# The order of weight conversions and half steps in an expert loop, branch hints at its groups, and a tail in pairs

## The chip, the cores and the metric

The kernel runs on one core of a Trainium2 chip. The metric is the device time of one execution in microseconds (us), the median of several runs; less is better.

## The reference

One decoder layer on 1024 tokens of width 1024, in float32: a conditioned normalisation, a mixer (a gated linear recurrence beside sparse attention), and a mixture of experts, which is what this case is about.

```python
N_EXPERTS = 64
TOP_K = 8
EXPERT_HIDDEN = 256

def swiglu(t, w_gu, w_dn):
    g, u = jnp.split(t @ w_gu, 2, axis=-1)
    return (jax.nn.silu(g) * u) @ w_dn
```

Each token goes through a shared expert and through the 8 of 64 experts that a router picks for it. An expert is `swiglu` with `w_gu` of 1024 x 512 and `w_dn` of 256 x 1024; its result is weighted, multiplied by a gate row and added to the token's row. The layer ends with an RMS normalisation of all rows with the gain `final_g`.

## The kernel before

**Columns, groups and kinds.** After the router, the tokens of every expert are packed into *columns*: a column is up to 128 tokens of one expert, a *half column* up to 64. The rows live in DRAM in `h2` (inputs) and `acc` (sums). Columns are put into *groups* of `x + y` columns of two experts: `x` of the one, whose weights stand in slot 0, `y` of the other, in slot 1. Groups of one shape are a *kind*; there are six, `KINDS`, each with `x`, `y`, whether the last column of either expert is a half column, and how many groups there may be. How many there are is known only at run time, so every kind is a nest of `tc.If(ns[kind] > k)` (L1830) around the bodies of its groups (L1831): the program falls through into group k while there is one, and jumps out past the whole nest when there is none. With the inputs of this case 27 groups run: ten of kind 0 (three columns and one, the last column of each expert a half), four of kind 1 (three and one, no half), eight of kind 2 (two and one, the last one a half), four of kind 3 (two and two, each expert's last a half), none of kind 4, one of kind 5 (one and one).

**A step** (`step`, L1961) handles one column. On TensorE (PE): the product of the rows `hTh`, `hTl` (the column's rows turned round, split into a high and a low part) with the weights `guh`, `gul` into `pG` (L1970, L1971, and L1976 if the column is full); in the middle of it, two transposes of the *previous* step's `t` into `pA` (L1926); then the eight transposes of the *next* column's rows `g` into `pX` (L1914, in `turn`); then the down product of the *previous* step, `tTh`, `tTl` with `dnh`, `dnl`, into `pY` (L126 to L128, or L1945 and L1946 for a half). VectorE (DVE) and ScalarE (ACT) split what PE needs: `hTh` (ACT, L1919) and `hTl` (DVE, L1920) from `pX`, `tTh` and `tTl` from `pA` (L1931, L1932), and of the weights, for each piece of 128 x 1024, the high part on ACT (L1904) and the low on DVE (L1905). They also form `t`, the silu of one half of `pG` times the other (for a half column: copy `u` on ACT L1981, two additions on DVE L1983, silu on ACT L1984, multiplication on DVE L1985), and the weighted output `y` (L1952 to L1958).

**The order.** Every engine runs its queue in the order written. The six pieces of a slot's weights (q0 to q3 of `w_gu`, q4 and q5 of `w_dn`) are loaded by SyncE into `raw`, and each is converted at a fixed place: `SPLITTING` has for every step of a group two strings, the pieces that are converted after the `gu` product is issued (`now`) and those at the step's end (`late`). `a4`, `a5` are left from the group before, `b0` to `b5` are the second expert's of this group, `n0` to `n5` the first expert's of the next. GpSimd (POOL) gathers rows for a later column (L1880) and adds the outputs into `acc` (L1886), one after another.

**The end.** After the last kind a drain ends the last column, and `final` (L2004 on) loads `acc` in eight tiles `xl`, takes the sums of squares on ACT (L2019), the inverse roots on DVE in a chain of small operations (L136 to L141), scales in three groups of three, three and two tiles (L2029 to L2032) and stores (L2034).

Of the kernel before, what the change touches and what calls it, by code (L numbers as in the profile page):

```python
# [7 lines left out]
F32 = mybir.dt.float32  # L8
# [3 lines left out]
AF = mybir.ActivationFunctionType  # L12
OP = mybir.AluOpType
# [4 lines left out]
D = 1024  # L18
T = 1024
NT = 8  # L20
KT = 8
EPS = 1e-6
# [5 lines left out]
         (2, 2, (True, True), 32, 276, 4), (2, 2, (False, False), 32, 132, 4), (1, 1, (False, False), 32, 406, 2))  # L28
S1, S2, S3, S4, S5, S6 = (x[4] for x in KINDS)
NC = 474  # L30


def turned(x):
# [6 lines left out]
def consts():  # L40
# [27 lines left out]
    pad = np.stack([1024 + p, 0 * p], 1).reshape(256)  # L68
    row = np.concatenate([low, e * 1024 + 1, pad, np.arange(NC)]).astype(f)[None]
    j = np.arange(4)  # L70
# [11 lines left out]
def flip(x, i):  # L82
# [25 lines left out]

SPLITTING = {(3, 1): ("a4 a5", "b0", "b1 b2", "b3", "b4", "b5 n0", "n1 n2", "n3"),
# [3 lines left out]


ORDER = (3, 2, 1, 0, 4, 5, 6, 7)
# [2 lines left out]
class K:  # L120
# [77 lines left out]
    def pool(self, st, name, bufs, **k):  # L198
        return st.enter_context(self.tc.tile_pool(name=name, bufs=bufs, reuse_waits="tile", **k))
# [741 lines left out]
    def rows(self):  # L941
# [7 lines left out]
        G.memset(self.sacc, 0.0)  # L949
        self.krow = row(a["k_row"], 384 + NC, "krow")  # L950
        self.g1r = row(self.mods[0:1], D, "g1r")
# [528 lines left out]
    def chain(self, t):  # L1480
# [209 lines left out]
        yield  # L1690
        hot = t.tile([128, 4, NC], F32R, name="hot")
        for j in range(4):
            V.tensor_scalar(hot[:, j], self.krow[:, 384:384 + NC], col[:, j:j + 1], None, op0=OP.is_equal)

        def look(rows, *parts):

            ps = psum()[:rows, :NC]
            n = len(parts) * 4
# [35 lines left out]
    def phase3(self, ctx):  # L1734
        tc, nc, a = self.tc, self.nc, self.a
        V, S, G, P = nc.vector, nc.scalar, nc.gpsimd, nc.tensor
        pool = self.pool
        big = ExitStack()
# [3 lines left out]
        with tc.manual_schedule():  # L1742
# [45 lines left out]
            m = pool(big, "moe", 1, side="right")  # L1788
# [4 lines left out]
            self.y = [m.tile([128, D], F32, name=f"y{s}") for s in range(2)]  # L1793
            self.idx = m.tile([128, NC], I32, name="idx")
            self.wgt = m.tile([128, NC], F32, name="wgt")
# [10 lines left out]
            tail = ExitStack()  # L1806
# [21 lines left out]
            ns = [nc.values_load(self.num[0:1, k:k + 1], min_val=0, max_val=KINDS[k][3]) for k in range(6)]  # L1828
            for kind, (_, _, half, most, c0, way) in enumerate(KINDS):
                with ExitStack() as nest:  # L1830
                    for k in range(most):  # L1831
                        self.prev = self.last(64 if k and half[1] else 128)
                        nest.enter_context(tc.If(ns[kind] > k))
                        self.group(kind, c0 + k * way)
            self.prev = self.last(128)
            self.drain()
            tail.close()
            self.final(pool(big, "last", 1, side="right"))
            big.close()

    def group(self, kind, c):
# [7 lines left out]
        f = {f"a{k}": self.todo[k] for k in (4, 5)}  # L1849
        at = iter(SPLITTING[x, y])  # L1850
        for u, (slot, cols) in enumerate(units):
# [109 lines left out]
    def step(self, slot, load, now, late, store, half=False, ahead=False):  # L1961


        nc = self.nc
        V, S, G, P = nc.vector, nc.scalar, nc.gpsimd, nc.tensor
        s = self.par
        gu = self.W[slot][0][0], self.W[slot][1][0]
        hT, ps = self.hT2[s], self.pG[s]
        for k in range(KT):
            P.matmul(ps, hT[0][:, k], gu[0][:, k], start=(k == 0), stop=False)  # L1970
            P.matmul(ps, hT[0][:, k], gu[1][:, k], start=False, stop=(half and k == KT - 1))  # L1971
            if k == 1 and self.prev:
                self.middle()
        if not half:
            for k in range(KT):
                P.matmul(ps, hT[1][:, k], gu[0][:, k], start=False, stop=(k == KT - 1))  # L1976
        for f in now:
            f()
        if half:
            t, u = self.t[:64], self.u  # L1980
            S.activation(u, ps[64:], AF.Copy)  # L1981
            for c in (slice(0, 256), slice(256, 512)):
                V.tensor_tensor(u[:, c], u[:, c], ps[:64, c], op=OP.add)  # L1983
            S.activation(t, u[:, :256], AF.Silu)  # L1984
            V.tensor_tensor(t, t, u[:, 256:], op=OP.mult)  # L1985
            self.turn(1 - s, ahead)
        else:
            S.activation(self.t, ps[:, :256], AF.Silu)
            V.tensor_tensor(self.t, self.t, ps[:, 256:], op=OP.mult)
            self.turn(1 - s, ahead)  # L1990
        if load:
            load(self.g[1 - s])
        if self.prev:
            self.down(self.pslot)
        for f in late:
            f()
        self.prev, self.pslot = store, slot
        self.par = 1 - s
# [5 lines left out]
    def final(self, m):  # L2004

        nc = self.nc
        V, S, G = nc.vector, nc.scalar, nc.gpsimd
        tok = [slice(i * 128, (i + 1) * 128) for i in range(NT)]
        self.fg = self.bcast(m, self.a["final_g"].rearrange("(a n) -> a n", a=1), D, "fg")
        xs = [m.tile([128, D], F32, name=f"xl{i}") for i in range(NT - 2)] + self.g  # L2010
        for i in range(NT):
            nc.sync.dma_start(xs[i], self.acc[tok[i]])
        groups = (0, 1, 2), (3, 4, 5), (6, 7)
        sums = [m.tile([128, len(tiles)], F32, name=f"ss{j}") for j, tiles in enumerate(groups)]
        r = {}

        def squares(j):
            for u, i in enumerate(groups[j]):
                S.activation(self.pY, xs[i], AF.Square, accum_out=sums[j][:, u:u + 1])  # L2019

        def root(j):
            ss = sums[j]
            V.tensor_scalar(ss, ss, 1.0 / D, EPS, op0=OP.mult, op1=OP.add)
            r[j] = self.rsqrt(m, ss, len(groups[j]), f"fr{j}")

        def scale(j):
            for u, i in enumerate(groups[j]):
                if u == 2:
                    S.activation(xs[i], xs[i], AF.Copy, scale=r[j][:, u:u + 1])  # L2029
                    G.tensor_tensor(xs[i], xs[i], self.fg, op=OP.mult)  # L2030
                else:
                    V.scalar_tensor_tensor(xs[i], xs[i], r[j][:, u:u + 1], self.fg, op0=OP.mult, op1=OP.mult)  # L2032
            for i in groups[j]:
                nc.sync.dma_start(self.out[0, tok[i]], xs[i])  # L2034

        squares(0)
        squares(1)
        root(0)
        scale(0)
        squares(2)  # L2040
        root(1)
        scale(1)
        root(2)
        scale(2)


def body(tc, a, out, dbg=None, upto=9):
# [33 lines left out]
```

## Time and profile before

| | us |
|---|---|
| median of 3 runs (2010.75 to 2018.43) | 2016.76 |
| the profiled execution | 2016.18 |
| its span in the trace | 2014.4 |
| expert groups, from the start of the first to the end of the last | 1037 to 1979 |
| the tail, from the last scatter to the end | 1980.8 to 2014.4 |

The profile is of one execution. Busy time is given by engine; PE's weight loads (PEld) overlap its matmuls. In its rows a name after an L is a line of the kernel, `out<-in` the tiles written and read, and "[1.25 <-ACT hTh L1919]" means that the engine had stood idle for 1.25 us until that instruction released it. "DVEq" and "PEldq" stand for an engine's sequencer: an engine that is named so was released by a branch or semaphore instruction.

### The profile page before, as it was taken

The page shows a single profiled execution, that of the slowest core. Times are in us where ns is not written, and L with a number is a line of the kernel's source. Part 1 is how long each engine was busy: PE and PEld are TensorE (multiplying, and loading weights), DVE is VectorE, ACT ScalarE, POOL GpSimd, SP SyncE. Part 2 cuts the span into 40 slices and gives each one's busy share as a digit, 9 for nine tenths or more (in the row PEclk, how much of TensorE's full clock was granted, in tenths as well). Part 3 has the DMA queues.
Part 4 walks back from the last instruction along what each step waited for, and adds up shares of the span by engine and source line. Part 5 has one row for each costly group of instructions (what it writes and reads, how often), then busy time and mean ns, then how long its engine had stood idle before and what let it go on. Part 6 is the DMA issues. An engine that isn't in the chain of part 4 may idle for free. (4 is left out here: it accounts for less than half of the span.)

```text
span 2014.4 us, 29910 instructions
## 1 busy us (share of the span) xinstructions
PE 1795.7 (89%) x10534; PEld 1519.9 (75%) x10534; DVE 1416.7 (70%) x2397; ACT 1002.8 (50%) x1685; POOL 759.9 (38%) x644
## 2 busy tenths in 40 slices
PE   3989889899998999997899898998999999989972
PEld 3878879898887799886777777776887777766751
DVE  5577687624866676655767888887676788877765
ACT  4544545433743454444135556564454666655542
POOL 5155666612234443323523333333333333333322
PEclk9999998999999899998999999998999999999986
DMA  7413242332411111104489888886986999978855
GB/s 252 129 50 108 63 129 92 96 114 85 159 63 43 43 43 38 38 12 144 77 262 286 269 235 261 239 263 174 300 252 169 357 313 301 290 241 251 235 156 195
DMA packets 184279, 343.80 MB, mean 171 GB/s; under 512 B 24508, under 2 KB 83136, under 8 KB 184064
## 3 DMA queue, kind: packets, MB, share of 16 engines
q1 hardware_dynamic: 154768, 268.82, 39.5%
q0 software_dynamic: 29200, 72.41, 16.2%
q8 instruction: 95, 1.56, 0.3%
q14 instruction: 120, 0.98, 0.2%
q10 hardware_dynamic: 96, 0.02, 0.0%
HBM read 300.72 MB, written 65.36 MB: 182 GB/s over the span
## 5 line engine op out<-in xcount | busy, mean ns | idle before, releaser
L1970 PE MATMUL pG<-guh,hTh 128*128 128x512 f32 x848 | 353.9, 417 | 64.0 <-ACT hTh L1919 33.9
L1971 PE MATMUL pG<-gul,hTh 128*128 128x512 f32 x848 | 344.1, 406 | 15.2 <-DVE gul L1905 14.2
L1886 POOL DMA_INDIRECT acc<-y,idx x71 | 146.7, 2066 | 353.6 <-DVE dnl L1905 88.6
L1905 DVE TENSOR_TENSOR gul<-raw,guh 128x1024 fp32r<-128x1024 f32 x224 | 267.2, 1215 | 2.1 <-ACT guh L1904 2.1
L1970 PEld LDWEIGHTS pG<-guh,hTh 128*128 128x128 f32 x848 | 164.1, 194 | 107.3 <-ACT hTh L1919 44.0
L1904 ACT ACTIVATE guh<-raw 128x1024 fp32r<-128x1024 f32 x224 | 229.0, 1050 | 3.1 <-DMA raw<-w_exp_gu 2.5
L1971 PEld LDWEIGHTS pG<-gul,hTh 128*128 128x128 f32 x848 | 164.4, 194 | 58.1 <-DVE gul L1905 26.0
L127 PE MATMUL pj<-wl,hTh 128*128 128x256 f32 (+1 forms) x576 | 165.2, 287 | 5.8 <-DVE wl L224 5.8
L126 PE MATMUL pj<-wh,hTh 128*128 128x256 f32 (+1 forms) x576 | 169.5, 294 | 0.2 <-ACT wh L223 0.2
L1880 POOL DMA_INDIRECT g<-h,idx x101 | 117.6, 1165 | 135.1 <-PE pX L1914 113.4
L128 PE MATMUL pj<-wh,hTl 128*128 128x256 f32 (+1 forms) x576 | 164.6, 286 | 0.0
L1295 PE MATMUL po<-v,pT 128*128 128x64 f32 x1056 | 137.9, 275 | 11.0 <-DVE ob L1309 6.6
L1263 ACT ACTIVATE p<-ps,nm 128x640 f32<-128x640 f32 (+7 forms) x128 | 89.9, 702 | 114.6 <-DVE nm L1261 112.8
L1295 PEld LDWEIGHTS po<-v,pT 128*128 128x128 f32 x1056 | 132.8, 194 | 15.4 <-issue 6.6
L1976 PE MATMUL pG<-guh,hTl 128*128 128x512 f32 x560 | 141.5, 394 | 0.0
L1905 DVE TENSOR_TENSOR dnl<-raw,dnh 128x1024 fp32r<-128x1024 f32 x110 | 132.9, 1232 | 2.1 <-ACT dnh L1904 2.1
L1920 DVE TENSOR_TENSOR hTl<-pX,hTh 128x1024 fp32r<-128x1024 f32 x71 | 86.9, 1224 | 58.7 <-ACT hTh L1919 54.2
L1976 PEld LDWEIGHTS pG<-guh,hTl 128*128 128x128 f32 x560 | 105.4, 188 | 24.9
L126 PE MATMUL pY<-dnh,tTh 128*128 128x512 f32 x292 | 123.0, 421 | 0.5 <-ACT tTh L1931 0.5
L128 PE MATMUL pY<-dnh,tTl 128*128 128x512 f32 x292 | 117.2, 402 | 0.0
L127 PEld LDWEIGHTS pj<-wl,hTh 128*128 128x128 f32 x576 | 111.6, 194 | 6.8 <-DVE wl L224 6.7
L127 PE MATMUL pY<-dnl,tTh 128*128 128x512 f32 x292 | 115.8, 396 | 0.0
(486 smaller groups left out, 4394.5 us busy)
## 6 DMA issues: line engine op xcount, KB each, us to landing
raw<-w_exp_gu SPq DMA_DIRECT2D x220, 512.0 KB
raw<-w_exp_dn SPq DMA_DIRECT2D x110, 512.0 KB
raw<-w_ada SPq DMA_DIRECT2D x24, 1024.0 KB
x<-x SPq DMA_DIRECT2D x16, 512.0 KB
raw<-w_in SPq DMA_DIRECT2D x16, 512.0 KB
raw<-w_in SPq DMA_DIRECT2D x5, 1024.0 KB
acc<-x SPq DMA_DIRECT2D x9, 512.0 KB
h<-y SPq DMA_DIRECT2D x8, 512.0 KB
```

The source lines that it names most:

```text
L126: mm(ps, l[0], r[0], start=first, stop=False)
L127: mm(ps, l[0], r[1], start=False, stop=False)
L128: mm(ps, l[1], r[0], start=False, stop=last)
L1263: nc.scalar.activation(p[:, :n], ps[:, :n], AF.Exp, bias=nm, accum_out=self.st[i]["sums"][:, h, br + 1:br + 2])
L1295: self.nc.tensor.matmul(self.po[:, h % 2, br], pt[:, u * 128:(u + 1) * 128], self.vst[br][:, a + u, g * 64:g * 64 + 64], start=(u == 0), s ...
L1880: return lambda g: nc.gpsimd.indirect_dma_start(out=g[:n, :], out_offset=None, in_=self.h2, in_offset=off, bounds_check=T - 1, oob_is_err= ...
L1886: return lambda y: nc.gpsimd.indirect_dma_start(out=self.acc, out_offset=off, in_=y[:n, :], in_offset=None, compute_op=OP.add, bounds_chec ...
L1904: S.activation(h[:, o:o + 1024], x, AF.Copy)
L1905: V.tensor_tensor(l[:, o:o + 1024], x, h.bitcast(F32)[:, o:o + 1024], op=OP.subtract)
L1970: P.matmul(ps, hT[0][:, k], gu[0][:, k], start=(k == 0), stop=False)
L1971: P.matmul(ps, hT[0][:, k], gu[1][:, k], start=False, stop=(half and k == KT - 1))
L1976: P.matmul(ps, hT[1][:, k], gu[0][:, k], start=False, stop=(k == KT - 1))
```

## The change

Five edits:

1. `SPLITTING`: in groups of 3 + 1, step 3 converts b4 now and n0, n1 late, step 4 n2, n3 now and b5 late; before, step 3 had b4 now, b5 and n0 late, step 4 n1, n2 now and n3 late. The other shapes change likewise.
2. In a half step, `turn` (the transposes and conversion of the next column's rows) is written ahead of the silu and the multiplication that form `t`.
3. Every `tc.If` gets a label, and each but a nest's last is followed by a branch hint for the next one, on five engines, with a register that is 1 when the program will jump at that next `If`, 0 when it will go on into its group. On every engine this puts two instructions behind the branch of a group: a comparison and the hint.
4. The pool `last` is opened before the drain, and the last `y` gets a tile of its own.
5. `final` loads and stores by the SyncE and ACT queues in turn, takes all squares first, and works in four pairs on DVE, with no scaling on ACT and POOL.

```diff
-SPLITTING = {(3, 1): ("a4 a5", "b0", "b1 b2", "b3", "b4", "b5 n0", "n1 n2", "n3"),
-             (2, 1): ("a4 a5 b0", "b1", "b2 b3", "b4 n0", "b5 n1 n2", "n3"),
-             (2, 2): ("a4 a5", "b0", "b1 b2", "b3", "b4 b5", "n0", "n1 n2", "n3"),
-             (1, 1): ("a4 a5 b0 b1", "b2 b3", "b4 b5 n0 n1", "n2 n3")}
+SPLITTING = {(3, 1): ("a4 a5", "b0", "b1 b2", "b3", "b4", "n0 n1", "n2 n3", "b5"),
+             (2, 1): ("b0 a4 a5", "b1", "b2 b3", "n0 n1", "n2 n3", "b4 b5"),
+             (2, 2): ("b0 a4 a5", "b1", "b2 b3", "n0", "b4 b5", "n1", "n2 n3", ""),
+             (1, 1): ("b0 b1 b2", "b3 a4 a5", "n0 n1 n2", "n3 b4 b5")}
...
-                        nest.enter_context(tc.If(ns[kind] > k))
+                        nest.enter_context(tc.If(ns[kind] > k, label=f"{kind}.{k}"))
+                        if k + 1 < most:
+                            tc.mark_branch_hint_location(f"{kind}.{k + 1}", hint=ns[kind] <= k + 1, engines=ENGINES)
                         self.group(kind, c0 + k * way)
             self.prev = self.last(128)
+            tail.close()
+            m = pool(big, "last", 1, side="right")
+            self.y[self.par] = m.tile([128, D], F32, name="yl")
             self.drain()
-            tail.close()
-            self.final(pool(big, "last", 1, side="right"))
+            self.final(m)
...
+            self.turn(1 - s, ahead)
             S.activation(t, u[:, :256], AF.Silu)
             V.tensor_tensor(t, t, u[:, 256:], op=OP.mult)
-            self.turn(1 - s, ahead)
...
-            nc.sync.dma_start(xs[i], self.acc[tok[i]])
-        groups = (0, 1, 2), (3, 4, 5), (6, 7)
...
+            (nc.sync, nc.scalar)[i % 2].dma_start(xs[i], self.acc[tok[i]])
+        pairs = [(i, i + 1) for i in range(0, NT, 2)]
+        sums = [m.tile([128, 2], F32, name=f"ss{j}") for j in range(NT // 2)]
+        for j, tiles in enumerate(pairs):
+            for u, i in enumerate(tiles):
                 S.activation(self.pY, xs[i], AF.Square, accum_out=sums[j][:, u:u + 1])
...
+        for j, tiles in enumerate(pairs):
+            V.tensor_scalar(sums[j], sums[j], 1.0 / D, EPS, op0=OP.mult, op1=OP.add)
+            r = self.rsqrt(m, sums[j], 2, f"fr{j}")
+            for u, i in enumerate(tiles):
+                V.scalar_tensor_tensor(xs[i], xs[i], r[:, u:u + 1], self.fg, op0=OP.mult, op1=OP.mult)
+                (nc.sync, nc.scalar)[u].dma_start(self.out[0, tok[i]], xs[i])
```

What stands on DVE in a group of kind 0, from the late conversions of its third step to the end of its fourth, the half step (`raw` to `gul` or `dnl` is a weight conversion, `u` and `t` are the half step's products, `hTl` the next column's rows, `y` the previous column's output). Before:

```order
L1905 TENSOR_TENSOR dnl_9407<-raw_10470,dnh_9406 128x1024
L1905 TENSOR_TENSOR gul_10479<-raw_9599,guh_10478 128x1024
L1932 TENSOR_TENSOR tTh<-pA,tTh 128x2x64
L1905 TENSOR_TENSOR gul_10479<-raw_9599,guh_10478 128x1024 x2
L1983 TENSOR_TENSOR u<-u,pG_9394 64x256 x2
L1985 TENSOR_TENSOR t<-t,u 64x256
L1920 TENSOR_TENSOR hTl_9564<-pX,hTh_9563 128x1024
L1953 TENSOR_TENSOR y_9572<-y_9572,pY 64x1024
L1954 SCALAR_TENSOR_TENSOR y_9572<-y_9572,wgt,g2r 64x1024
L1905 TENSOR_TENSOR gul_10479<-raw_9599,guh_10478 128x1024
```

The same place on DVE with the change:

```order
L1910 TENSOR_TENSOR gul_10479<-raw_9599,guh_10478 128x1024 x2
L1937 TENSOR_TENSOR tTh<-pA,tTh 128x2x64
L1910 TENSOR_TENSOR gul_10479<-raw_9599,guh_10478 128x1024 x2
L1988 TENSOR_TENSOR u<-u,pG_9394 64x256 x2
L1925 TENSOR_TENSOR hTl_9564<-pX,hTh_9563 128x1024
L1991 TENSOR_TENSOR t<-t,u 64x256
L1958 TENSOR_TENSOR y_9572<-y_9572,pY 64x1024
L1959 SCALAR_TENSOR_TENSOR y_9572<-y_9572,wgt,g2r 64x1024
L1910 TENSOR_TENSOR dnl_9407<-raw_10470,dnh_9406 128x1024
```

The `dnl` conversion has gone from the first place to the last, all four `gul` conversions stand ahead of the additions, and `hTl` stands ahead of the multiplication that ends `t`.

On ACT, the same half step before:

```order
L1931 ACTIVATE tTh<-pA 128x2x64
L1904 ACTIVATE guh_10478<-raw_9599 128x1024 x2
L1981 ACTIVATE u<-pG_9394 64x512
L1984 ACTIVATE t<-u 64x256
L1919 ACTIVATE hTh_9563<-pX 128x1024
L1952 ACTIVATE y_9572<-pY 64x1024
L1904 ACTIVATE guh_10478<-raw_9599 128x1024
```

And on ACT with the change:

```order
L1936 ACTIVATE tTh<-pA 128x2x64
L1909 ACTIVATE guh_10478<-raw_9599 128x1024 x2
L1986 ACTIVATE u<-pG_9394 64x512
L1924 ACTIVATE hTh_9563<-pX 128x1024
L1990 ACTIVATE t<-u 64x256
L1957 ACTIVATE y_9572<-pY 64x1024
L1909 ACTIVATE dnh_9406<-raw_10470 128x1024
```

`hTh`, which the next step's first matmul reads, now stands ahead of the silu `t<-u`, which waits for DVE's additions.

DVE at the start of kind 0's second group, where the hints come in. Before:

```order
L1830 COMPARE_AND_BRANCH
L1932 TENSOR_TENSOR tTh<-pA,tTh 128x2x64
L1905 TENSOR_TENSOR dnl_10481<-raw_9599,dnh_10480 128x1024 x2
L1989 TENSOR_TENSOR t<-t,pG_9393 128x256
L1920 TENSOR_TENSOR hTl_9566<-pX,hTh_9565 128x1024
```

And with the change:

```order
L1831 COMPARE_AND_BRANCH
L1836 REGISTER_ALU
L2061 BRANCH_PREFETCH_HINT
L1937 TENSOR_TENSOR tTh<-pA,tTh 128x2x64
L1910 TENSOR_TENSOR dnl_10481<-raw_9599,dnh_10480 128x1024 x2
L1994 TENSOR_TENSOR t<-t,pG_9393 128x256
```

Behind the branch stand the comparison and the hint, the same on each of the five engines, and then the group as before.

More of the change, by code (lines that the diff above doesn't have):

```diff
@@ L30 @@
 NC = 474
+ENGINES = [getattr(mybir.EngineType, x) for x in ("PE", "Activation", "DVE", "Pool", "SP")]
 def turned(x):
@@ L2011, in final @@
         for i in range(NT):
-            nc.sync.dma_start(xs[i], self.acc[tok[i]])
-        groups = (0, 1, 2), (3, 4, 5), (6, 7)
[L2014 to L2044, printed above, removed]
+            (nc.sync, nc.scalar)[i % 2].dma_start(xs[i], self.acc[tok[i]])
[3 more added lines that the diff above has]
+            for u, i in enumerate(tiles):
+                S.activation(self.pY, xs[i], AF.Square, accum_out=sums[j][:, u:u + 1])
+        for j, tiles in enumerate(pairs):
[4 more added lines that the diff above has]
+                (nc.sync, nc.scalar)[u].dma_start(self.out[0, tok[i]], xs[i])
 def body(tc, a, out, dbg=None, upto=9):
```

## The prediction

> **What bounds the kernel now.** I read the page first (busy time), then PE's waits in the expert stage, then the busy time by stretches, one group of each kind, and last the order of time at the stalls.
>
> ```profile
> span 2014.4 us, 29910 instructions
> PE 1795.7 (89%) x10534; PEld 1519.9 (75%) x10534; DVE 1416.7 (70%) x2397; ACT 1002.8 (50%) x1685; POOL 759.9 (38%) x644
> ```
>
> PE is busy 89% of the span, the others far less. Next, whom PE waited for from 1037 to 1979 us, the expert stage (sum, how often, the longest):
>
> ```profile
> PE pG L1970 <- ACT hTh L1919: 31.7, 22, 1.6
> PE pG L1970 <- DVEq L1830: 29.5, 4, 12.6
> PE pG L1971 <- DVE gul L1905: 14.2, 11, 2.2
> PE pA L1926 <- DVEq L1830: 3.8, 1, 3.8
> ```
>
> And five stretches of that stage (length, then busy time with counts of PE, weight load, DVE, ACT, POOL, then PE's clock, DMA share, GB/s): a group of kind 0, one of kind 1, the first of kind 2, another of kind 2, one of kind 3.
>
> ```profile
> 1284.30:1319.70 35.40, 32.85 (x163) 25.75 (x162) 29.01 (x37) 20.78 (x28) 12.60 (x8) 1.00 0.85 249
> 1437.50:1475.40 37.90, 37.90 (x187) 31.06 (x185) 26.78 (x31) 18.56 (x25) 12.40 (x8) 1.00 0.90 258
> 1558.60:1583.40 24.80, 24.76 (x113) 19.92 (x114) 15.71 (x18) 13.71 (x18) 5.52 (x5) 0.93 1.01 345
> 1666.70:1694.50 27.80, 26.11 (x128) 20.56 (x127) 24.37 (x30) 17.89 (x24) 8.97 (x6) 1.00 0.98 306
> 1857.70:1894.40 36.70, 33.49 (x162) 25.44 (x161) 29.05 (x37) 20.78 (x28) 14.08 (x9) 1.00 0.81 238
> ```
>
> PE is the bound, full in kind 1 (37.90 of 37.90) and with 2.55, 1.69 and 3.21 us of holes in kinds 0, 2 and 3. The wait rows name the holes: 31.7 us for `hTh` in 22 places, 14.2 us for `gul` in 11, and 33.3 us (29.5 + 3.8) at the five places where the program jumps out of a kind's nest. All else that the change touches is the tail. The time to be won in the expert stage is these 79 us and no more.
>
> **The half step.** What its stall is made of, in order of time, where kind 0's half step passes into the next group:
>
> ```profile
> 1178.13 2.35 DVE L1905 TENSOR_TENSOR gul<-raw,guh 128x1024 fp32r<-128x1024 f32 x2
> 1178.19 1.03 PE L1914 MATMUL pX<-ident,g 128*128 128x128 f32 x8
> 1180.40 0.74 DVE L1983 TENSOR_TENSOR u<-u,pG 64x256 f32<-64x256 f32 x2
> 1180.71 0.40 PE L1946 MATMUL pY<-dnl,tTh 128*128 128x512 f32 x1
> 1180.84 0.42 ACT L1984 ACTIVATE t<-u 64x256 f32<-64x256 f32 x1 [1.86 <-DVE u L1983]
> 1181.28 1.02 ACT L1919 ACTIVATE hTh<-pX 128x1024 fp32r<-128x1024 f32 x1
> 1181.29 0.42 DVE L1985 TENSOR_TENSOR t<-t,u 64x256 f32<-64x256 f32 x1 [0.15 <-ACT t L1984]
> 1182.34 1.23 DVE L1920 TENSOR_TENSOR hTl<-pX,hTh 128x1024 fp32r<-128x1024 f32 x1 [0.63 <-ACT hTh L1919]
> 1182.36 0.50 PE L1970 MATMUL pG<-guh,hTh 128*128 128x512 f32 x1 [1.25 <-ACT hTh L1919]
> 1183.39 0.38 PE L1926 MATMUL pA<-ident,t 128*128 128x128 f32 x2
> 1184.72 1.28 DVE L1954 SCALAR_TENSOR_TENSOR y<-y,wgt,g2r 64x1024 f32<-64x1024 f32 x1
> 1185.92 1.21 DVE L1905 TENSOR_TENSOR gul<-raw,guh 128x1024 fp32r<-128x1024 f32 x1
> 1187.18 0.50 PE L1971 MATMUL pG<-gul,hTh 128*128 128x512 f32 x1 [1.31 <-DVE gul L1905]
> ```
>
> `pX` is ready at 1179.22, but `hTh` stands on ACT behind the silu, which waited 1.86 us for the `u` adds, themselves behind two conversions on DVE. So `hTh` ends at 1182.30 and PE, done at 1181.11, waits 1.25. With the turn moved ahead, `hTh` runs at 1179.3 to 1180.3 and this wait is gone. What is late next is `t`: DVE does `hTl` (1.23) ahead of the multiplication. The adds end at 1181.14, `hTl` at 1182.37, `t` (0.42) at 1182.8 or, with the 0.05 to 0.15 us that such handovers take, 1182.95. PE, starting at 1181.11, reaches `pA` after the 1.03 us that lie between 1182.36 and 1183.39, at 1182.14: a **new wait of 0.8 us** where there was none. Net gain 1.25 - 0.8 = 0.45.
>
> **The order of the pieces.** The last row's 1.31 us is n3's `gul`, converted late, behind `hTl` and the two `y` operations (1184.72 to 1186.0). In the new order n2 and n3 stand together ahead of the adds, where the old order also had two conversions (the 2.35), and b5, a `dn` piece wanted only by the down product of the next step, takes the late place. So this wait goes without a successor. Kind 0 has ten groups (1037 to 1390.4), nine boundaries inside: 9 x (0.45 + 1.31) = **15.8 us**. Bounds: 0, if another wait fills both, and 23 (9 x 2.56), if `t` isn't late.
>
> **Kind 2.** Its eight groups have seven such boundaries:
>
> ```profile
> 1660.54 1.46 POOL L1886 DMA_INDIRECT acc<-y,ci  x1 [6.35 <-DMA acc<-y,idx]
> 1662.73 1.28 DVE L1958 SCALAR_TENSOR_TENSOR y<-pY,wgt,g2r 128x1024 f32<-128x1024 f32 x1 [1.21 <-PE pY L128]
> 1671.89 0.50 PE L1970 MATMUL pG<-guh,hTh 128*128 128x512 f32 x1 [1.61 <-ACT hTh L1919]
> ```
>
> 7 x 1.61 = 11.3 us, here with no new wait, since `n2 n3` no longer stand between the adds and `t`. But the stretch row has DMA at 0.98 of 27.80 us: if those 27.2 us can't shrink, 0.6 a boundary is all, 4.2 us. Against that, the kind's first group moved 345 GB/s, 13% over the 306 of the stretch, which would carry the whole 1.61. I take **7**, between the ends 4.2 and 11.3.
>
> **Kind 3 and kind 1.** What is left of the 31.7 us is 31.7 - 11.25 - 11.3 = 9.2 us at six half steps of kind 3, 1.5 each; by the sum above each keeps a `pA` wait of 0.8 to 1.1, which leaves **2.5** to 4 us; I take the lower, as these steps carry two half columns. Kind 1 has no half step and PE without a hole: 0.
>
> **The exits.** PE stops there while DVE runs its queue dry. The branches of all five places and of the groups between (count, least, middle and longest ns):
>
> ```profile
> L1830 PEldq COMPARE_BRANCH  x38: 65/65/5802, 1037.0 to 1969.0; - x38
> L1830 DVEq COMPARE_BRANCH  x38: 43/43/67, 1042.2 to 1972.6; - x38
> ```
>
> And the first exit in order of time:
>
> ```profile
> 1392.78 0.40 PE L1946 MATMUL pY<-dnl,tTh 128*128 128x512 f32 x1
> 1399.19 0.14 DVE L1864 COPY cw<-wgt 128x1 f32<-128x1 f32 x1
> 1400.23 0.76 PE L1970 MATMUL pG<-guh,hTh 128*128 128x512 f32 x1 [7.06 <-DVEq L1830]
> ```
>
> PE's branch takes 65 ns when it falls through into the next group and up to 5.8 us when it jumps. The jump hides behind DVE: its last instruction ends at 1399.33, PE goes on at 1400.23. Even a free jump gains 0.9 us here, and about 3.7 over the five places. The new order shifts one late conversion (1.2 us) into kind 2's exit and one out of kind 3's: 0 net. The added instructions (one compare, one hint, for each of 27 groups and engine) at 65 ns each come to 3.5 us if nothing hides them; PE's sequencer runs ahead of its matmuls, so I take **0** for their issue, bounds 0 and +3.5. [...]
>
> **The tail.**
>
> ```profile
> 1988.33 1.03 ACT L2019 ACTIVATE pY<-xl 128x1024 f32<-128x1024 f32 x1
> 1991.76 0.17 DVE L2023 TENSOR_SCALAR ss<-ss 128x3 f32<-128x3 f32 x1 [11.26 <-DMA xl<-acc]
> 1996.73 2.33 DVE L136 TENSOR_SCALAR fr1t<-ss 128x3 int32<-128x3 int32 x1
> 2001.06 4.65 DVE L2032 SCALAR_TENSOR_TENSOR xl<-xl,fr1y,fg 128x1024 f32<-128x1024 f32 x2
> 2007.99 2.48 DVE L2032 SCALAR_TENSOR_TENSOR g<-g,fr2y,fg 128x1024 f32<-128x1024 f32 x2
> ```
>
> Now three roots (some 2.37 us each, 1991.76 to 1994.14) and six scalings end at 2010.47. After, with pairs, the chain starts two squares in (1989.6, the second ends at 1989.36), and holds 4 x 2.37 + 8 x 1.24 = 19.4 us on DVE, so it ends at 2009.0, **-1.4**; the 2.17 us on each of two DVE operations that ran beside POOL's multiplication (2.33 where its like took 0.17, 4.65 where it took 2.48) go with POOL's part. Opening the last pool ahead of the drain, with a tile of its own for the last `y`, moves nothing that I can see, since the loads read `acc` and so wait for the last scatter as before: 0. Two queues for eight loads may land the first pair later; bounds -2 and +1, taken **-1**. [...]
>
> **Sum.** 15.8 + 7 + 2.5 + 1 = 26 us from the profiled execution's 2016.2 (the median of the runs is 2016.8, 0.03% off, so no correction): 1990. The scatters, next, can hold some of it back; I leave 3 us for them: **1993**, own range 1982 (2016.2 - 23 - 11.3, kinds 0 and 2 at their bounds) to 2003 (half the sum).
>
> **Rivals.**
>
> [...]
>
> [...]
>
> [...]
>
> *The scatters take the stall's place.* POOL's additions into `acc` go one after the other: at 1660.54 it waited 6.35 us for the scatter before, and the next `y` is written at 1662.73, 2.2 us behind. If the scatter chain, not PE, sets the period of kind 2 and the half groups, only that margin is won, once, with half of the `gul` waits of kind 0 (9 x 1.31 / 2 = 5.9) and the tail: 2016.2 - 2.2 - 5.9 - 1 = **2007**. For it: every kind 2 scatter waits for a landing. Against it: PE's row names no wait for `y`.
>
> *The jumps become short* because the hints bring the target in: 3.7 us more, **1989**. For it: PE's jumps are 3.6 to 5.8 us. Against it: DVE, not PE, ends last there; and the sense of the register would have to be the other.
>
> *The hints do nothing* is the forecast itself.
>
> **How the numbers follow.** Forecast 0.43, short jumps 0.07, scatters 0.16, code loading 0.34. About 0.5%, or 10 us, is what a measurement of this kernel can tell from no change: 2006 to 2026 counts as same. Faster: 0.42 + 0.07 + 0.04 = 0.53; same: 0.01 + 0.10 + 0.05 = 0.16; slower: 0.02 + 0.29 = 0.31. The range goes down to the forecast's lower bound with the short jumps' 3.7 us, 1982 - 4 = 1978, and up into the code loading case as far as leaves out no more than 2 in 10: 2046.
>
> **What would show it.** Right: `hTh` waits gone, `pA` waits of 0.8 us on `t` in kind 0, `gul` waits gone but for the first, kind 0 groups at 33.6 us, kind 2 near 26.8. [...] Scatters: PE or ACT waiting for `acc<-y`. It would be wrong from the start if `t` or the new late b5 comes much later than counted.

## The result, and the profile after

The changed kernel takes 1983.78 us in the median of four runs (1979.6 to 1984.11), the kernel before 2016.71 in the same measurement: a ratio of 0.984, 95% interval 0.982 to 0.986. The profiled execution took 1979.6 us, the fastest of the four. Its page:

```profile
span 1977.8 us, 30098 instructions
PE 1785.2 (90%) x10534; PEld 1517.6 (77%) x10534; DVE 1409.0 (71%) x2411; ACT 999.0 (51%) x1683; POOL 755.6 (38%) x642
```

PE's busy time is 10.5 us less for the same 10534 matmuls. PE's waits in the expert stage (who waited for whom, sum, how often, the longest):

```profile
PE pG L1975 <- DVEq L1831: 24.4, 4, 10.9
PE pA L1931 <- DVE t L1991: 12.5, 16, 1.3
PE pA L1931 <- DVEq L1831: 5.7, 1, 5.7
PE pX L1919 <- DMA g<-h,idx: 4.2, 2, 2.3
PE pY L1950 <- DVE tTh L1937: 3.0, 1, 3.0
PE pY L129 <- DVE tTl L1937: 2.8, 1, 2.8
PE pG L1976 <- DVE gul L1910: 2.6, 2, 2.2
PE pA L1931 <- DVE t L1994: 1.4, 1, 1.4
```

The 31.7 us for `hTh` are gone without a rest, the `gul` waits but for the first and one of 0.4 us in kind 5. New are sixteen `pA` waits for the `t` of a half step, one for that of a full column, and two single waits of about 3 us, which the section on the hints takes up. The stretches of a group of kind 0, one of kind 2, one of kind 3, and of the fifth group of kind 0 (length, busy time and counts of PE, weight load, DVE, ACT, POOL, then PE's clock, DMA share, GB/s):

```profile
1276.25:1309.34 33.09, 32.47 (x161) 25.79 (x161) 28.51 (x37) 20.67 (x29) 11.95 (x8) 1.00 0.86 264
1667.50:1693.16 25.66, 25.66 (x128) 20.63 (x127) 24.09 (x30) 17.85 (x23) 8.35 (x5) 1.00 0.99 323
1797.55:1832.15 34.60, 32.84 (x160) 25.55 (x160) 28.74 (x37) 20.79 (x28) 11.92 (x9) 1.00 0.90 252
1172.98:1210.05 37.07, 32.71 (x160) 25.81 (x161) 28.64 (x37) 20.66 (x29) 13.52 (x10) 1.00 0.87 253
```

The groups went from 35.4, 27.8 and 36.7 us to 33.1, 25.7 and 34.6, and PE's rows fill all 25.66 us of kind 2's group. The order of time where kind 0's half step passes into the next group:

```profile
1305.94 1.03 ACT L1924 ACTIVATE hTh<-pX 128x1024 fp32r<-128x1024 f32 x1 [0.28 <-PE pX L1919]
1307.08 0.74 DVE L1988 TENSOR_TENSOR u<-u,pG 64x256 f32<-64x256 f32 x2
1307.62 0.40 PE L1975 MATMUL pG<-guh,hTh 128*128 128x512 f32 x1
1307.74 1.21 DVE L1925 TENSOR_TENSOR hTl<-pX,hTh 128x1024 fp32r<-128x1024 f32 x1
1308.32 0.40 PE L1976 MATMUL pG<-gul,hTh 128*128 128x512 f32 x1
1308.87 0.41 DVE L1991 TENSOR_TENSOR t<-t,u 64x256 f32<-64x256 f32 x1
1309.34 0.44 PE L1931 MATMUL pA<-ident,t 128*128 128x128 f32 x2 [0.62 <-DVE t L1991]
```

`hTh` is done at 1306.97, 0.65 us before PE reads it; `t` is what PE now waits for, behind `hTl`: 0.62 to 0.67 us at eight of the nine boundaries of kind 0, and 1.32 us at the one behind the group of 37.07 us.

### The profile page after: what moved, and what is told of

Its sections match the earlier page's. It is cut to its first block, busy times and chain, and to the rows that moved or that the text cites. A ratio compares the mean times of both kernels' runs of the same rounds, so it can differ in the third digit from the quotient of the medians.

```text
span 1977.8 us, 30098 instructions
## 1 busy us (share of the span) xinstructions
PE 1785.2 (90%) x10534; PEld 1517.6 (77%) x10534; DVE 1409.0 (71%) x2411; ACT 999.0 (51%) x1683; POOL 755.6 (38%) x642
## 5 line engine op out<-in xcount | busy, mean ns | idle before, releaser
L1975 PE MATMUL pG<-guh,hTh 128*128 128x512 f32 x848 | 349.8, 413 | 27.2 <-DVEq L1831 24.4
L1976 PE MATMUL pG<-gul,hTh 128*128 128x512 f32 x848 | 339.9, 401 | 2.6 <-DVE gul L1910 2.6
L1885 POOL DMA_INDIRECT g<-h,idx x101 | 125.1, 1239 | 118.5 <-PE pX L1919 92.5
L1936 ACT ACTIVATE tTh<-pA 128x256 fp32r<-128x256 f32 (+1 forms) x106 | 37.2, 351 | 163.8 <-PE pA L1931 141.4
```

The costliest lines, as they stand in the source:

```text
L1885: return lambda g: nc.gpsimd.indirect_dma_start(out=g[:n, :], out_offset=None, in_=self.h2, in_offset=off, bounds_check=T - 1, oob_is_err= ...
```

## The experiments

The table holds every kernel: its median, the ratio to the kernel before on the same chip with its 95% interval, and in its single trace the length of the expert stage, from the end of PE's first `gul` wait to the `pA` transposes behind the last exit. What lies ahead of that stage is the same code in all, and yet the stage begins anywhere from 1036 to 1043 us in these traces; so its length is a cleaner measure of a single trace than the span. It scatters too: e9 has the same code in that stage as the kernel before, and its stage is 3.8 us shorter. Medians of different rows may come from different chips; rows are compared by their ratios.

| kernel | median us | ratio (interval) | expert stage us |
|---|---|---|---|
| before | 2014.4 to 2017.1 | 1 | 932.4 |
| the change | 1983.8 | 0.984 (0.982 to 0.986) | 899.5 |
| e1 change without hints | 1974.1 | 0.981 (0.979 to 0.983) | 892.3 |
| e2 before, hints alone | 2033.6 | 1.010 (1.008 to 1.012) | 945.3 |
| e3 change, hints reversed | 1966.8 | 0.977 (0.975 to 0.978) | 885.6 |
| e4 before, turn alone | 1994.3 | 0.990 (0.989 to 0.992) | 908.5 |
| e5 change, hints always 1 | 1975.6 | 0.980 (0.978 to 0.983) | 893.0 |
| e6 change, no hints on DVE | 1973.6 | 0.979 (0.977 to 0.982) | 890.1 |
| e7 change, hints on DVE alone | 1989.3 | 0.986 (0.984 to 0.988) | 906.8 |
| e8 before, pieces and turn | 1977.1 | 0.982 (0.979 to 0.984) | 890.3 |
| e9 before, tail alone | 2016.9 | 1.000 (0.999 to 1.001) | 928.6 |
| e10 before, pieces alone | 1993.1 | 0.989 (0.987 to 0.990) | 906.8 |
| e11 e3 with `t` ahead of `hTl` | 1958.6 | 0.972 (0.970 to 0.973) | 872.4 |
| e12 e11 without hints | 1964.5 | 0.975 (0.973 to 0.977) | 884.9 |

### The hints

Three theories stood after the result: the hints do nothing; they pay, since PE's jumps had become short (0.35 to 0.38 us at the exits of kinds 0 to 3, where 3.6 to 5.8 had been); they cost, since DVE had stood still twice inside a group (3.89 us at 1203 and 3.98 at 1643). "Late code" in the expectations is the author's guess at what DVE stood still for; no row shows it. **e1** leaves them out:

```diff
-                        nest.enter_context(tc.If(ns[kind] > k, label=f"{kind}.{k}"))
-                        if k + 1 < most:
-                            tc.mark_branch_hint_location(f"{kind}.{k + 1}", hint=ns[kind] <= k + 1, engines=ENGINES)
+                        nest.enter_context(tc.If(ns[kind] > k))
```

> The changed kernel without its hints (edits 1, 2, 4 and 5 alone). If the hints do nothing for the time, 1984 us. If they pay by the short jumps, it is slower by what the exits lost in the changed kernel's trace, about 3 us: 1987, with PE's branch at 3.6 to 5.8 us again at every exit and PE's holes there back to 7.1, 3.9, 6.0 and 12.6 us. If they cost by late code, it is faster: DVE stood still twice for 3.9 us in the middle of a group (at 1203 and 1643 us) with all its operands there, and without hints both stops are gone, 1976.

**e2** is the kernel before with the hints of the change and nothing else.

> The kernel before with the hints alone. Hints nothing: 2016.7. Short jumps pay: 2013, PE's branches at the exits of kinds 0 to 3 under 0.4 us and the holes there shorter. Late code: 2020 to 2025, with stops of DVE of about 4 us inside groups.

**e3** turns the register's sense round in the changed kernel:

```diff
-hint=ns[kind] <= k + 1
+hint=ns[kind] > k + 1
```

> The changed kernel with the sense of the hint's register turned: 1 where the program goes on, 0 where it jumps. If 1 means 'bring in the target', as the short jumps of the changed kernel suggest, 22 hints are now wrong: PE stops inside groups, 2 us each in the middle, 2025 or so, and the jumps take 3.6 to 5.8 us again. If the register's value does nothing, it equals the changed kernel: 1984.

Without hints the kernel is some 6 us faster by the ratios, 0.981 against 0.984, but their intervals overlap a little. The kernel before makes it plain: hints alone cost it 1.0%, some 20 us, with the whole interval above 1, and more than the 2020 to 2025 us expected. So in the change the hints cost, and the other edits gave more than the result shows. e3 came out against its expectation, both of whose branches gave at least the time of the change: the reversed sense is faster than no hints at all, 0.977 against 0.981. Whether PE's jumps are short is read from its branches. At the exit of kind 0 (count, least, middle and longest ns), in the changed kernel:

```profile
L1831 PEldq COMPARE_BRANCH  x3: 65/190/382, 1372.7 to 1376.0; - x3
```

in e1:

```profile
L1831 PEldq COMPARE_BRANCH  x3: 73/193/3365, 1370.5 to 1374.4; - x3
```

and in e3:

```profile
L1831 PEldq COMPARE_BRANCH  x3: 65/195/421, 1368.1 to 1371.4; - x3
```

Both senses make that jump short, 0.38 and 0.42 us against 3.4. Kind 5 tells them apart, since only one of its groups runs and so only one hint. The change, where that hint has the value 1:

```profile
L1831 PEldq COMPARE_BRANCH  x2: 193/3140/6086, 1928.5 to 1934.8; - x2
```

e3, where it has 0:

```profile
L1831 PEldq COMPARE_BRANCH  x2: 186/277/368, 1915.1 to 1918.9; - x2
```

With 1 the jump took 6.1 us, with 0 0.37, and without hints (e1) 5.9. So **0 is the value that makes the jump short**. In the change the 22 groups that go on have the value 0 and the last group of each kind has 1; the jumps behind the last groups of kinds 0 to 3, each with zeros in the groups before, were short all the same, 0.35 to 0.38 us. **e5** puts this to the test, with the same instructions at the same places but the value always 1:

```diff
-hint=ns[kind] <= k + 1
+hint=ns[kind] <= 40
```

> The changed kernel with the hint's register always 1, so the same instructions at the same places, but in no group the value 0. If the value decides and 0 means 'bring in the target of the jump', this does nothing: the time of the kernel without hints, 1974, with PE's jumps at 3.4 to 5.9 us again. If it is the shifted code or the extra instructions that made the reversed hints 7 us faster than none, it is 1967. If 1 also loads something, PE or DVE stop inside groups: 1984.

It equals no hints, 0.980 against 0.981, with stage lengths 893.0 and 892.3, and its jumps are long again (5.9 us in kind 5). So neither the extra instructions nor the shifted code make a difference that this measurement can tell: the value does. **e6** and **e7** ask which engine pays, with these lines:

```diff
-engines=ENGINES
+engines=[e for e in ENGINES if e != mybir.EngineType.DVE]
```

and

```diff
-engines=ENGINES
+engines=[mybir.EngineType.DVE]
```

> The changed kernel with its hints on PE, ACT, POOL and SP, none on DVE. If the cost of the 22 hints with 0 is DVE's late code alone, the stops are gone: 1974, or 1972 with short jumps on the other engines. If the other engines' code is late too, it stays near 1984; in between, each takes its share.

> The changed kernel with its hints on DVE alone. If DVE's late code is the cost: 1982 to 1984, stops of DVE of about 4 us inside groups, PE's jumps long. If the cost is elsewhere: 1974 or less.

The cost is DVE's: without its hints 0.979, with them alone 0.986, intervals well apart. That e7 lies above the change itself and above the 1982 to 1984 us expected may mean that the other engines' hints give something back there; the intervals of e7 and of the change overlap, so it is not shown. Three stops in the changed kernel, DVE's rows (the second row is the last work ahead of the second stop):

```profile
1125.99 1.28 DVE L1963 SCALAR_TENSOR_TENSOR y<-pY,wgt,g2r 128x1024 f32<-128x1024 f32 x1 [3.28 <-PE pA L1931]
1197.88 1.28 DVE L1963 SCALAR_TENSOR_TENSOR y<-pY,wgt,g2r 128x1024 f32<-128x1024 f32 x1 [1.33 <-PE pY L129]
1203.05 2.36 DVE L1910 TENSOR_TENSOR gul<-raw,guh 128x1024 fp32r<-128x1024 f32 x2 [3.89 <-ACT u L1986]
1642.95 2.36 DVE L1910 TENSOR_TENSOR gul<-raw,guh 128x1024 fp32r<-128x1024 f32 x2 [3.98 <-DMA raw<-w_exp_gu]
```

The same places in e7:

```profile
1132.80 1.28 DVE L1963 SCALAR_TENSOR_TENSOR y<-pY,wgt,g2r 128x1024 f32<-128x1024 f32 x1 [4.18 <-issue]
1209.75 2.36 DVE L1910 TENSOR_TENSOR gul<-raw,guh 128x1024 fp32r<-128x1024 f32 x2 [4.03 <-ACT u L1986]
1649.07 2.36 DVE L1910 TENSOR_TENSOR gul<-raw,guh 128x1024 fp32r<-128x1024 f32 x2 [3.91 <-ACT u L1986]
```

And e2, where another conversion stands behind the same `y`, again in the fifth group of kind 0:

```profile
1210.12 1.23 DVE L1908 TENSOR_TENSOR dnl<-raw,dnh 128x1024 fp32r<-128x1024 f32 x1 [4.09 <-ACT u L1984]
1293.17 1.21 DVE L1956 TENSOR_TENSOR y<-y,pY 64x1024 f32<-64x1024 f32 x1 [4.46 <-issue]
```

And ACT in the changed kernel, ahead of the stop at 1203.05:

```profile
1195.68 2.00 ACT L1909 ACTIVATE guh<-raw 128x1024 fp32r<-128x1024 f32 x2
```

DVE's `y` ended at 1199.16 and its conversion began at 1203.05, though ACT had written `guh` for it by 1197.68; the releasers named (ACT's `u`, PE's `pA`, a DMA) are only what happened last, and twice it is "issue", that is, nothing that the profile shows. The change and e7 stop at the same instructions of the same groups, a `y` in kind 0's third group, a `gul` in its fifth and a `gul` in one group of kind 2. The other groups of kind 0 pass these instructions without such a stop, and e1, e5 and e6 pass all three places (the same `y` waits 1.2 us in e1, for PE). That speaks for a place in the code, not for the data. What DVE's sequencer waited for, no row shows; that its next code was late there is the author's guess, and fits.

### The orders

**e4** has edit 2 alone (the turn ahead of the silu), **e10** edit 1 alone (`SPLITTING`), **e8** both, each on the kernel before.

```diff
+            self.turn(1 - s, ahead)
             S.activation(t, u[:, :256], AF.Silu)
             V.tensor_tensor(t, t, u[:, 256:], op=OP.mult)
-            self.turn(1 - s, ahead)
```

> The kernel before with edit 2 alone (the turn ahead of the silu in half steps). By the theory that a recorded wait of 1.25 to 1.6 us costs 0.3 to 0.5 us more than its length: kind 0 loses the hTh wait and gets a pA wait of 0.6, and keeps the gul wait of 1.3 (net 0.9 x 9); kind 2 has a third conversion ahead of its additions, so t is late there and only 0.8 of 2.1 is won (x 7); kind 3 as in the changed kernel (5): 1998. If the waits cost no more than their length: 2003. If the scatters hold kind 2, its groups stay at 27.8 us and it is 2005 or more.

> The kernel before with edit 1 alone (order of pieces). The gul wait of kind 0 goes (9 x 1.3 and 0.2 for each restart), the hTh waits stay in kinds 0 and 3 and are shorter in kind 2, whose last step no longer has three conversions ahead of the additions (1.6 to 0.4): 2015 - 13.5 - 8.4 = 1993. If the hTh wait grows by as much as the gul wait shrinks, it stays at 2010 or more.

> The kernel before with edits 1 and 2 (order of pieces, turn ahead of the silu). By the traces the tail's edits gave 2 us and the hints none or a loss: 1976, with kind 0 groups of 33.1 us and kind 2 groups of 25.7. If the tail's edits gave more, for instance by the early opening of the last pool, it is slower than 1978; if the piece order needs the turn, it is more than edit 2 alone (1994) and much less here.

The turn alone gives 1.0% (19 us), the pieces alone 1.1% (23 us), both 1.8% (37 us): they nearly add up, and they are the whole gain of the change. PE's waits show which stall each removes. In e4 the 22 `hTh` waits have become `pA` waits for `t`, and the `gul` waits stay:

```profile
PE pA L1926 <- DVE t L1986: 17.4, 22, 1.0
PE pG L1971 <- DVE gul L1905: 11.8, 11, 2.2
```

In e10 only the first `gul` wait is left, and the `hTh` waits stay, shorter in kind 2:

```profile
PE pG L1970 <- ACT hTh L1919: 23.8, 21, 1.5
PE pG L1971 <- DVE gul L1905: 2.2, 1, 2.2
```

e4's theories were worked out from 2016.7 us. Its ratio puts it at 1997 from there, the first theory's 1998, and clear of the two others (2003 and 2005): a wait costs more than its recorded length. How much more is read at one boundary of kind 2 in the kernel before:

```profile
1669.65 0.39 PE L127 MATMUL pY<-dnl,tTh 128*128 128x512 f32 x1
1669.88 0.40 PE L128 MATMUL pY<-dnh,tTl 128*128 128x512 f32 x1
1671.89 0.50 PE L1970 MATMUL pG<-guh,hTh 128*128 128x512 f32 x1 [1.61 <-ACT hTh L1919]
1672.22 0.40 PE L1971 MATMUL pG<-gul,hTh 128*128 128x512 f32 x1
1675.01 0.39 PE L1970 MATMUL pG<-guh,hTh 128*128 128x512 f32 x1
1675.47 0.50 PE L1971 MATMUL pG<-gul,hTh 128*128 128x512 f32 x1
1675.81 0.40 PE L1970 MATMUL pG<-guh,hTh 128*128 128x512 f32 x1
```

The second row is the last matmul ahead of the wait. From its start to that of the next it is 2.01 us, where matmuls of this size follow each other at 0.23 in the same group: 1.78 us lost, because the recorded end is modelled at 0.40 after the start and the wait is counted from there. The matmul behind the stop follows at 0.33 instead of 0.23, another 0.1. So this stop cost some 1.9 us instead of 1.61. The group shrank by 2.12; the rest fits a second, short stop 3.6 us later, where PE waited for a `gul` that DVE ended at 1675.42: 0.46 and 0.34 instead of 0.23, of which the recorded ends show a gap of 0.07 us.

### The tail

**e9** has edits 4 and 5 alone.

> The kernel before with edits 4 and 5 alone (early pool, tail in pairs). By the changed kernel's trace, from the last scatter to the end 31.7 us instead of 33.6: 2013.2, 2 us less than the kernel before. If the gain of the tail was due to the earlier groups (a shorter queue of scatters), nothing: 2015.

No difference, 1.000 (0.999 to 1.001), which leaves room for 2 us either way, and not the 2 us less that were expected from the change's trace. From the last scatter to the end its trace has 32.9 us (1979.65 to 2012.6), the kernel before 33.6, the changed kernel 31.7 (1946.14 to 1977.8).

### A faster kernel

In **e11** the half step's `t` is finished on DVE between `hTh` and `hTl`, on top of e3; **e12** is e11 without hints.

```diff
         nc.scalar.activation(h, x, AF.Copy)
+        if mult:
+            silu()
+            mult()
         nc.vector.tensor_tensor(l, x, h.bitcast(F32), op=OP.subtract)
...
-            self.turn(1 - s, ahead)
-            S.activation(t, u[:, :256], AF.Silu)
-            V.tensor_tensor(t, t, u[:, 256:], op=OP.mult)
+            self.turn(1 - s, ahead, lambda: V.tensor_tensor(t, t, u[:, 256:], op=OP.mult), lambda: S.activation(t, u[:, :256], AF.Silu))
```

> The changed kernel with the hints' sense reversed and, in half steps, DVE's multiplication that ends t written between hTh and hTl, so that pA no longer waits behind hTl. It should win the pA waits of kinds 0 and 3 with what each restart costs, 9 x 0.8 + 6 x 1.05 = 13.5 us, from the 1967 of the reversed hints: 1954. If hTl, now 0.4 us later, is late for PE in its turn, less: 1960 to 1967.

> The kernel of e11 without hints. With the other order the reversed hints gave 7 us (e1 against e3), of which the single traces show 1.7 at the exits and 4.2 at gathers that came late behind two exits. If the hints pay at the exits and just behind them: ratio about 0.975 (7 us above e11's 0.9715), with waits for gathered rows after the exits. If they don't, and the 7 us were the luck of a trace or of where the code lies: 0.9715.

PE's waits in e11, all but one of 0.5 us:

```profile
PE pG L1978 <- DVEq L1831: 22.7, 4, 7.3
PE pA L1934 <- DVEq L1831: 5.4, 1, 5.4
PE pX L1919 <- DMA g<-h,idx: 2.8, 2, 1.5
PE pG L1979 <- DVE gul L1910: 2.2, 1, 2.2
```

The `pA` waits for `t` are gone and nothing has come in their place: inside the groups PE no longer waits, and 28.1 of the 33.6 us that are left lie at the exits. The stage is 13.2 us shorter than e3's, as expected (13.5). By ratio 0.972 stands against 0.977, 11 us; the median of 1958.6 is above the expected 1954, on another chip, whose kernel before took 2.4 us longer too. This is the fastest of all, 2.8% below the kernel before. e12 is 0.3% slower, 6 us, as expected, with the ends of the intervals just overlapping. Its waits:

```profile
PE pG L1976 <- DVEq L1831: 25.2, 4, 7.8
PE pX L1917 <- DMA g<-h,idx: 10.3, 2, 8.5
PE pA L1932 <- DVEq L1831: 5.4, 1, 5.4
```

The differences are 2.5 us at the exits and 7.5 at gathered rows, which POOL orders only after its own jump (at kind 0's exit in the change its branches end at 1389.11 and its gather starts at 1390.55); e1 against e3 had the same pattern, 1.6 and 4.4. One trace each doesn't prove the gathers, whose waits vary, but the two pairs agree in direction and size.

## Why the prediction held, point by point

The direction was right, and so was the mechanism of the gain, the waits for `hTh` and `gul`; the time (1983.8 against 1993) lies 9 us under the forecast and 6 us above the lower end of the range. Two steps were off by 6 us and more, in opposite directions: the groups gained 16 us more than the sum had, and the hints cost 6 to 9 that it had at nothing. That the number came out as near as it did is partly luck.

**The `hTh` stall and its successor: right.** All 22 waits went, and `pA` waits for `t` came, of 0.62 us in kind 0 where 0.8 was worked out, and 0.9 in kind 3 (0.8 to 1.1).

**The pieces: right.** The `gul` waits of kind 0 left no successor; b5, late now, was waited for by nobody.

**The size of a gap: too small.** The sum took 1.75 us for each boundary of kind 0, 1.0 in kind 2 and 2.5 us for kind 3. Measured from the group lengths it was 2.3 (35.4 to 33.1), 2.1 (27.8 to 25.7), and 2.1 for each of three group lengths of kind 3. So 9 x 2.3 + 7 x 2.1 + 3 x 2.1 = 41.7 us in place of 15.8 + 7 + 2.5 = 25.3; e8 measured 37. The step that failed is the term "a wait costs its recorded length": at the boundary of kind 2 shown above the stop costs 0.17 us more, since the end of the matmul ahead of it is modelled, and 0.1 by the matmul behind it. In kind 0 the same figures make 1.25 + 1.31 - 0.62 + 0.27 = 2.2 of the 2.3 us. In kind 2 the cap by the DMA share fell as well: at a share of 0.99 the queues moved 323 GB/s instead of 306, and PE's rows filled the group. In kind 3 the recorded waits fell by 1.3 us a group (1.55 + 1.50 to 0.90 + 0.87) and the group by 2.1; the pieces alone (e10) shorten it by 0.7 with `hTh` waits as long as before, by stops that no wait row shows.

**The hints at nothing: wrong.** They cost 6 to 9 us in the change (by the ratios of e1, e5 and e6; each interval only just meets that of the change) and 20 on the kernel before. The chance of 0.34 for code loading, and with it the range's upper end of 2046, stood for a stop of PE of some 2 us in each of the 22 groups whose register is 0: an estimate of the author's, which no run shows. What the runs show in its place is DVE standing still in a few places, for 3.3 to 4.5 us each (the change, e7 and e2), and PE waiting behind it. That DVE's branches take 67 ns at most (the row in the prediction) does not say that a jump costs DVE nothing. Two rows of DVE's sequencer in the kernel before, its second jump at kind 3's exit and its next event of any sort:

```profile
L1830 DVEq COMPARE_BRANCH  x1: 63/63/63, 1940.1 to 1940.1; - x1
L1830 DVEq EVENT_SEMAPHORE  x1: 21/21/21, 1946.0 to 1946.0; - x1
```

The 5.9 us between them, in which DVE has no row, are nearly half of PE's 12.6 at that exit. So there the forecast's reading, that PE stops while DVE runs its queue dry, was wrong: DVE's last work ended at 1938.76, and PE went on at 1946.21. e6 and e7 put the cost of the hints on DVE (0.979 and 0.986). It stays open why it is DVE's and not PE's, and why the hints on ACT and POOL cost nothing that e6 shows.

**The short jumps, a rival given 3.7 us: they came, and gave little.** With the change, PE's jumps fell from 5.3, 4.1, 5.8 and 3.6 us to 0.4 at the exits of kinds 0 to 3, with the sense of the register that the rival took for the wrong one. Its waits there sum to 30.1 us in the change against 29.6 in e1, whose jumps are long: DVE ends last, as the forecast had it. Only with the sense reversed, on every engine (e3: 28.0), is there a gain.

**The scatters: right as an argument, and the 3 us left for them were not needed.** PE's waits name no `y` in any run.

**The exits at 0 and the tail at -1:** PE's waits at the exits fell from 33.3 to 30.1 us, but those for gathered rows, which follow the exits, rose from 0.7 to 4.2, so 0 held. That PE's sequencer runs ahead of its matmuls shows at the first exit of the kernel before: its branch starts at 1390.4, and the last matmul issued ahead of it ends at 1393.18. At kind 3's exit (12.6 to 10.9) DVE's work behind PE's last matmul shrank from 5.2 to 3.9 us, while from its second branch there to its next row still 6.1 us passed (1904.18 to 1910.25); in e1, without hints, PE's longest wait at an exit was 8.3. The tail measures 0, with -2 to +2 open, which neither breaks its bounds nor shows its sign.

What stays open: why the hints cost 20 us on the kernel before and less than half of that in the change, where the same number of hints stands at the start of the same groups. The traces hold only part of it: e2's stage is 12.9 us longer than that of the kernel before, with PE waits of 3.2, 5.9 and 2.8 us behind stops of DVE, where the change has two; and e2's profiled run, at 2023.9 us, was its fastest by 9.

## What to carry to other kernels

Write first, on each engine, what the bound engine reads next, and then ask what that pushes behind it: here `hTh` ahead of the silu won 1%, and `t` ahead of `hTl` another 0.5%. Price a stall of a pipelined engine from start to start of the instructions around it, not by the recorded wait (here 1.9 us, where 1.61 was recorded). A hint that helps one engine can hurt another: here the same value made PE's jumps short (0.35 to 0.38 us for 3.6 to 5.8) and DVE stop inside groups (3.3 to 4.2 us in the change and e7). Measure its value both ways and without it, engine by engine, before giving it to all.

## What the hardware showed unasked

At kind 5's exit PE's jump took 0.37 us with the hint's value 0 (e3), 6.1 with 1 (the change), 5.9 with 1 in every group (e5) and 5.9 without hints (e1); by ratio e5 equals e1, 0.980 against 0.981. At the exits of kinds 0 to 3 of the change the last hint ahead of the jump was 1 and those of the groups before it 0, and the jump was short, 0.35 to 0.38 us. What passes at a jump of DVE or POOL stands in no branch row: at kind 3's exit of the kernel before their branches last 37 to 63 ns, and between a branch and the engine's next row lie 5.9 us on DVE and 3.5 on POOL, for what, no row shows.
